# The opening of a decoder trunk: one accumulator per group of modulation columns, and scaling and rounding on ScalarE

## The chip, the cores and the metric

The kernel runs on one core of one Trainium2 chip. TensorE (PE) multiplies matrices, its loads of the stationary operand stand as PEld; Vector (DVE), ScalarE (ACT) and GpSimd (POOL) work on elements; SyncE (SP) issues every transfer here. Each engine runs its own queue in order and waits on semaphores for the others. The metric is device time in microseconds (us) of one execution. Before the change three runs took 1229.35 to 1232.19, median 1229.94.

## The reference

A trunk of two layers on 256 tokens of width 1024, all in float32. Every sublayer normalizes x, changes it by a shift and a scale that come from a vector c, computes (SwiGLU with 2816 hidden columns, attention, SwiGLU again), and adds a gated result to x. The part that this case is about is the start of the first SwiGLU:

```python
c_act = silu(c)
mod = (c_act @ mod_w[0] + mod_b[0])          # 9 vectors of 1024; shift and scale are the first two
h = rms_norm(x, norm_g) * (1 + scale) + shift
gate, up = h @ w_gate, h @ w_up              # then silu(gate) * up, and the product with w_down
```

## The kernel before, in words

Each float32 operand of a large product is kept as two parts: a rounded one (hTh for h, wh for weights) and the residue (hTl, wl). ScalarE rounds a weight tile of 128 x 1024 numbers, Vector subtracts to get the residue, and TensorE makes three products: wh with hTh, wh with hTl, wl with hTh.

The opening (open_trunk, line 672) must have h before it can multiply. It takes the 1024 input features in four groups of two columns of 128 (groups, k0 and n). For a group q, load_mod loads the rows of mod_w for shift and scale of these 256 features, eight tiles of 128 x 512 numbers (256 KB each, tag oraw), and load_weights loads three tiles of 512 KB: for each feature column k one with 512 columns of gate and 512 of up (key (0, k)), and one for both columns with the next 512 of gate (key (1, k), k even). The tag raw has four such tiles (RAWS).

reduce (line 751) multiplies the eight mod_w tiles by the eight columns of c and adds them up on Vector, in two accumulators (k even, k odd). modulate (line 763) sums each accumulator over its 128 partitions with TensorE, by matmuls with a column of ones; a float32 matmul of this kind shows as two instructions, so a group has sixteen. Then Vector makes shift and scale (tile sb) and h itself (hk), ScalarE rounds it to hTh, Vector makes hTl. split (line 739) rounds a weight tile and makes its residue. normalize (line 700) squares x on ScalarE, takes the root on GpSimd, scales x on Vector (tile u), transposes it on TensorE and copies it to xT on ScalarE. columns (line 685) turns rows into columns by one transpose and a Vector copy: for c, and for gain, shift bias and scale bias (gb8).

products (line 793) makes the twelve matmuls of a piece: one feature column k against 512 weight columns, in four blocks of 128, three kinds of product for each (mm_blocks, line 383). pieces lists a group's six: the gate and up halves of (0, k), those of (0, k+1), then the two columns of (1, k). The outputs stand in six PSUM banks until the end of the opening; two banks are left for transposes and column sums.

The order on every engine is the order in which the program writes the instructions: in the opening it is kept on PE, SP, DVE, ACT and POOL. For group q it is: the remaining reduces of q, the column sums, the first weight splits (OPEN_SPLIT of them, between), shift, scale and h, first reduces of q+1 (OPEN_MEAN, meanwhile), residues of h, the other splits, reduces of q+1 up to OPEN_HEAD; on TensorE the sums, the pieces held back of group q-1 (backlog, OPEN_HOLD: 3, 2, 2), then the pieces of q but for those held back. Behind the opening a planner orders DVE, ACT and POOL, and an instruction written later can come to run inside the opening. weights.start (line 191) begins the loads of the next phase when group 3 is reached.

Of the kernel before, what the change touches and what calls it, by code (L numbers as in the profile page):

```python
# [17 lines left out]
P = 128  # L18
# [6 lines left out]
H = 16  # L25
# [5 lines left out]
OPEN_HEAD = 4  # L31
OPEN_SPLIT = (2, 2, 2, 1)
OPEN_MEAN = (1, 2, 2)
OPEN_HOLD = (3, 2, 2)
# [57 lines left out]
def trunk_kernel(ctx, tc, x_in, c_in, positions, mod_w, mod_b, norm_g, w_gate, w_up, w_down,  # L92
# [62 lines left out]
    nc.gpsimd.memset(ones.bitcast(F32), 1.0)  # L155

# [228 lines left out]
    def mm_blocks(o, k, wh, wl, first, last):  # L385

        for i in range(4):
# [3 lines left out]
            pe.matmul(out_i, wl[:, blk], hTh[:, :, k, :], start=False, stop=last and i % 2 == 1)  # L391

# [278 lines left out]
    def open_trunk(wg, wu, pool):  # L671
# [28 lines left out]
        def normalize(t):  # L700
            ss = main.tile([P, 2], F32, tag="ss", bufs=4, name="ss")
            for h in range(2):
                square(t, h, slice(h * 512, (h + 1) * 512), ss)
            rs = rms_scale(ss)

            def half(h):
                xn = main.tile([P, 512], F32, tag="u", bufs=3, name="u")
                dve.tensor_scalar(xn, x[t][:, h * 512:(h + 1) * 512], rs, None, op0=OP.mult)
                tp = bank4()
                for k in range(4):  # L710
                    pe.transpose(tp[:, k, :], xn[:, k * P:(k + 1) * P], ident)
                act.copy(xT[:, t, h * 4:(h + 1) * 4, :], tp)

            return [lambda: half(0), lambda: half(1)]
# [10 lines left out]

        def load_weights(q):
            k0, n = groups[q]
            for k in range(k0, k0 + n):
                rows = slice(k * P, (k + 1) * P)
                raw = rawp.tile([P, 2, 512], F32, tag="raw", bufs=RAWS, name="raw")  # L730
# [3 lines left out]
                if k % 2 == 0:  # L734
                    raw = rawp.tile([P, 2, 512], F32, tag="raw", bufs=RAWS, name="raw")
                    nc.sync.dma_start(raw, wg[k * P:(k + 2) * P, 512:1024].rearrange("(k p) n -> p k n", p=P))
                    ws[1, k] = raw

        def split(key):
# [4 lines left out]
            dve.tensor_sub(wl, raw, wh.bitcast(F32))  # L744
            ws[key] = wh, wl
            uses[key] = 2
            weights.live += 1

        accs = {}

        def reduce(q, rows, extra=()):
            n = groups[q][1]
            for k in rows:
                if k < 2:
                    accs[q, k] = pool.tile([P, 2, 2 * P], F32, tag=f"cacc{k}", bufs=2, name=f"cacc{k}")[:, :, 0:n * P]
                    dve.tensor_scalar(accs[q, k], raws[q, k], ccol[:, k:k + 1], None, op0=OP.mult)
                else:
                    dve.scalar_tensor_tensor(accs[q, k % 2], raws[q, k], ccol[:, k:k + 1], accs[q, k % 2],
                                                   op0=OP.mult, op1=OP.add)
                if extra:  # L760
                    extra.pop(0)()

        def modulate(q, between, meanwhile):
            k0, n = groups[q]
            cp = bank()
            terms = [(accs[q, i], ones.bitcast(F32)[:, 0:1]) for i in range(2)]
            for j in range(2):
                for i in range(n):
                    for m, (a, c) in enumerate(terms):
                        pe.matmul(cp[:, n * j + i:n * j + i + 1], a[:, j, i * P:(i + 1) * P], c,  # L770
                                         start=m == 0, stop=m == len(terms) - 1)
            between()
# [5 lines left out]
            hk = pool.tile([P, NT, 2, P], F32, tag="hk", bufs=2, name="hk")  # L778
            for i in range(n):
                dve.tensor_scalar(hk[:, :, i, :], xT[:, :, k0 + i], sb[:, 1, i:i + 1], sb[:, 0, i:i + 1],  # L780
                                        op0=OP.mult, op1=OP.add)
            for t in range(NT):
                act.copy(hTh[:, t, ks, :], hk[:, t, 0:n])  # L783
            meanwhile()
# [633 lines left out]
```

## Time and profile before

| | |
|---|---|
| median of three runs | 1229.94 us |
| the profiled execution | 1230.24 us, its span 1228.5 us |
| TensorE busy | 1202.4 us, 98% |
| Vector busy | 936.6 us, 76% |
| ScalarE busy | 657.4 us, 54% |
| transfers | 281 MB, 229 GB/s over the span |

Times are counted from the start of the span. A busy TensorE is not TensorE at its peak: its matmuls overlap, so the pace, from one start to the next, says more than the duration of one. In a row of the timeline, the bracket is the idle time of that engine before the instruction and what released it.

### The profile page before, as it was taken

The numbers are of one execution on the slowest core, as the hardware profiler recorded it, in microseconds if no ns is written. First come the engines' busy times: TensorE is split into PE (matmuls) and PEld (weight loads), VectorE is DVE, ScalarE is ACT, GpSimd is POOL, SyncE is SP. The second block draws the span as 40 slices with busy tenths as digits, with TensorE's granted clock in tenths as the row PEclk, the third lists the DMA queues.
The fourth block names the chain that finished last, engine by engine and source line by source line (L and its number), as shares of the span: only waits on it lengthen the run. The fifth ranks groups of instructions, "written<-read, shape, count | busy, mean of one in ns | idle before, by whom it ended". The sixth has DMA issues, their size and how long they took to land.

```text
span 1228.5 us, 21017 instructions
## 1 busy us (share of the span) xinstructions
PE 1202.4 (98%) x8130; PEld 1085.5 (88%) x8130; DVE 936.6 (76%) x1318; ACT 657.4 (54%) x1002; POOL 101.9 (8%) x130
## 2 busy tenths in 40 slices
PE   6999999999999999999999999999999999999998
PEld 5999988878779999889999887888888787999987
DVE  7878777998788887579978659978686877765653
ACT  4446444676654554444554435677575665544540
POOL 1000000222100000000000003131131200000000
PEclk9999999999999999999999999999999999999999
DMA  9879885695739988638888647656545552866461
GB/s 334 277 269 327 304 317 182 199 306 201 272 99 341 330 275 310 206 111 292 305 277 325 206 154 235 210 181 211 175 154 182 197 173 86 289 203 217 168 213 42
DMA packets 152069, 281.21 MB, mean 229 GB/s; under 512 B 13424, under 2 KB 79504, under 8 KB 151968
## 3 DMA queue, kind: packets, MB, share of 16 engines
q1 hardware_dynamic: 151968, 279.85, 68.4%
q8 instruction: 64, 1.05, 0.3%
q14 instruction: 37, 0.30, 0.1%
HBM read 277.71 MB, written 2.10 MB: 228 GB/s over the span
## 4 chain that ended last, share of the span: by engine, by line
PE 76%; DVE 9%; DMA 5%; issue 4%; POOL 2%; ACT 2%; SPq 0%; POOLq 0%; DVEq 0%; ACTq 0%
PE block_bank L389 13%; PE block_bank L391 13%; PE block_bank L390 13%; PE bank L394 11%; PE bank L395 11%; PE bank L396 11%; DMA mraw<-in_mod_w_dram 3%; DVE wl L215 2%; POOL hrs L860 2%; DVE acc L296 1%; DVE lo L924 1%; PE obank L949 1%; DMA raw<-in_dil_w_in_dram 1%; DMA raw<-in_fox_w_in_dram 1%; ACT wh L206 1%
## 5 line engine op out<-in xcount | busy, mean ns | idle before, releaser
L215 DVE TENSOR_TENSOR wl<-raw,wh 128x1024 fp32r<-128x1024 f32 (+1 forms) x360 | 434.9, 1216 | 160.1 <-ACT wh L206 156.8
L206 ACT CAST wh<-raw 128x1024 fp32r<-128x1024 f32 (+1 forms) x360 | 374.5, 1046 | 299.2 <-PE bank L396 107.2
L389 PE MATMUL block_bank<-hTh,wh 128*128 128x256 f32 x1312 | 371.6, 283 | 2.0 <-ACT hTh L783 2.0
L391 PE MATMUL block_bank<-hTh,wl 128*128 128x256 f32 x1312 | 371.4, 283 | 0.0
L390 PE MATMUL block_bank<-hTl,wh 128*128 128x256 f32 x1312 | 370.7, 283 | 0.0
L389 PEld LDWEIGHTS block_bank<-hTh,wh 128*128 128x128 f32 x1312 | 248.5, 189 | 2.5 <-ACT hTh L783 2.1
L390 PEld LDWEIGHTS block_bank<-hTl,wh 128*128 128x128 f32 x1312 | 248.2, 189 | 0.5 <-DVE hTl L786 0.2
L391 PEld LDWEIGHTS block_bank<-hTh,wl 128*128 128x128 f32 x1312 | 248.0, 189 | 0.0
L394 PE MATMUL bank<-wh,hTh 128*128 128x512 f32 (+2 forms) x496 | 192.0, 387 | 0.8 <-DVE nm L924 0.8
L396 PE MATMUL bank<-wh,hTl 128*128 128x512 f32 (+2 forms) x496 | 181.6, 366 | 0.0
L395 PE MATMUL bank<-wl,hTh 128*128 128x512 f32 (+2 forms) x496 | 181.0, 365 | 0.0
L296 DVE SCALAR_TENSOR_TENSOR acc<-mraw,ccols,acc 128x1024 f32<-128x1024 f32 x112 | 143.4, 1281 | 29.8 <-DMA mraw<-in_mod_w_dram 29.3
L395 PE MATMUL bank<-wl,aTh 128*128 128x512 f32 (+1 forms) x420 | 146.4, 349 | 0.0
L394 PE MATMUL bank<-wh,aTh 128*128 128x512 f32 (+1 forms) x420 | 146.1, 348 | 0.0
L396 PE MATMUL bank<-wh,aTl 128*128 128x512 f32 (+1 forms) x420 | 145.7, 347 | 0.0
L396 PEld LDWEIGHTS bank<-wh,hTl 128*128 128x128 f32 x496 | 93.2, 188 | 16.5 <-DVE hTl L471 0.5
L394 PEld LDWEIGHTS bank<-wh,hTh 128*128 128x128 f32 x496 | 93.6, 189 | 14.0 <-DVE nm L924 1.2
L395 PEld LDWEIGHTS bank<-wl,hTh 128*128 128x128 f32 x496 | 93.7, 189 | 12.3
L394 PEld LDWEIGHTS bank<-wh,aTh 128*128 128x128 f32 x420 | 79.5, 189 | 10.8
L396 PEld LDWEIGHTS bank<-wh,aTl 128*128 128x128 f32 x420 | 79.3, 189 | 10.5
L395 PEld LDWEIGHTS bank<-wl,aTh 128*128 128x128 f32 x420 | 79.5, 189 | 10.1
L926 ACT ACTIVATE lo<-lo,nm 128x128 f32<-128x128 f32 (+1 forms) x64 | 37.8, 591 | 64.8 <-DVE nm L924 64.7
(225 smaller groups left out, 1280.9 us busy)
## 6 DMA issues: line engine op xcount, KB each, us to landing
mraw<-in_mod_w_dram SPq DMA_DIRECT2D x128, 512.0 KB, 5.2
raw<-in_ffn_w_down_dram SPq DMA_DIRECT2D x88, 512.0 KB, 4.1
raw<-in_ffn_w_gate_dram SPq DMA_DIRECT2D x76, 512.0 KB, 4.4
raw<-in_ffn_w_up_dram SPq DMA_DIRECT2D x76, 512.0 KB, 4.6
raw<-in_dil_w_in_dram SPq DMA_DIRECT2D x128, 256.0 KB, 4.2
raw<-in_fox_w_in_dram SPq DMA_DIRECT2D x36, 256.0 KB, 4.8
oraw<-in_mod_w_dram SPq DMA_DIRECT2D x32, 256.0 KB, 6.3
raw<-in_ffn_w_gate_dram SPq DMA_DIRECT2D x24, 256.0 KB, 6.0
```

Source lines behind the costliest of these rows:

```text
L206: act.copy(wh, self.raws[self.hi])
L215: dve.tensor_sub(wl, self.raws[self.lo], wh.bitcast(F32))
L296: dve.scalar_tensor_tensor(acc, raw, ccol[:, k:k + 1], self.bias_tile if k == 0 else acc, op0=OP.mult, op1=OP.add)
L389: pe.matmul(out_i, wh[:, blk], hTh[:, :, k, :], start=first and i % 2 == 0, stop=False)
L390: pe.matmul(out_i, wh[:, blk], hTl[:, :, k, :], start=False, stop=False)
L391: pe.matmul(out_i, wl[:, blk], hTh[:, :, k, :], start=False, stop=last and i % 2 == 1)
L394: pe.matmul(o, ah, wh, start=first, stop=False)
L395: pe.matmul(o, ah, wl, start=False, stop=False)
L396: pe.matmul(o, al, wh, start=False, stop=last)
L860: nc.gpsimd.tensor_tensor(rs, ms, mhalf, op=OP.pow)
L924: dve.tensor_tensor_reduce(out=lo[:, 0:n], in0=lg[:, 0:n], in1=m, scale=-1.0, scalar=BIG, op0=OP.add, op1=OP.min, accum_out=nm)
L926: act.activation(lo[:, 0:n], lo[:, 0:n], AF.Exp, bias=nm, scale=-1.0, accum_out=sums[:, t, i:i + 1])
```

## The change

What it does, part by part. reduce adds all eight tiles of a group into one accumulator; for groups 1 to 3 the first multiplication runs on ScalarE. The column sums have half as many passes. normalize scales x on ScalarE and copies up to three transposed halves later. The copy of the gain and bias columns is written behind the reduce of k = 4 of group 0. modulate, now a generator, rounds h on ScalarE straight from xT; the plain h is made by Vector in group 0 and by ScalarE in the others; residues of h are made by column. Splits are cut in two (split_hi on ScalarE, split_lo on Vector), and the adds of the next group are written between the residues of the weights: two ahead of each in groups 1 and 2, all behind them in group 0. Every third raw tile of the opening comes from a new tag with two tiles. Within a piece the matmuls are ordered by kind (mm_parts). One piece of each group is held back. A small constant (idr) is built at the front of the kernel.

```diff
@@ -28,10 +28,7 @@
...
 OPEN_GROUPS = (2, 2, 2, 2)
-OPEN_HEAD = 4
-OPEN_SPLIT = (2, 2, 2, 1)
-OPEN_MEAN = (1, 2, 2)
-OPEN_HOLD = (3, 2, 2)
+OPEN_HOLD = 1
 T_FOX = 2
@@ -154,6 +151,11 @@
...
+    idr = const.tile([CUM, H], F32R, name="idr")
+    nc.gpsimd.memset(idr.bitcast(F32), 0.0)
+    for r in (0, 2 * H):
+        dve.tensor_copy(idr[r:r + H, :], ident[r:r + H, r:r + H])
     mhalf = const.tile([P, 8], F32, name="mhalf")
@@ -389,6 +391,14 @@
...
             pe.matmul(out_i, wl[:, blk], hTh[:, :, k, :], start=False, stop=last and i % 2 == 1)
+    def mm_parts(o, k, wh, wl, first, last):
+        for w, h in ((wh, hTh), (wh, hTl), (wl, hTh)):
+            for i in range(4):
+                blk = slice(i * P, (i + 1) * P)
+                pe.matmul(o[i // 2][:, i % 2], w[:, blk], h[:, :, k, :], start=first and w is wh and h is hTh and
+                          i % 2 == 0, stop=last and w is wl and i % 2 == 1)
@@ -697,21 +707,27 @@
...
-        def normalize(t):
-            ss = main.tile([P, 2], F32, tag="ss", bufs=4, name="ss")
-            for h in range(2):
-                square(t, h, slice(h * 512, (h + 1) * 512), ss)
-            rs = rms_scale(ss)
-            def half(h):
-                xn = main.tile([P, 512], F32, tag="u", bufs=3, name="u")
-                dve.tensor_scalar(xn, x[t][:, h * 512:(h + 1) * 512], rs, None, op0=OP.mult)
-                tp = bank4()
-                for k in range(4):
-                    pe.transpose(tp[:, k, :], xn[:, k * P:(k + 1) * P], ident)
-                act.copy(xT[:, t, h * 4:(h + 1) * 4, :], tp)
-            return [lambda: half(0), lambda: half(1)]
+        def normalize():
+            rs = []
+            for t in range(NT):
+                ss = main.tile([P, 2], F32, tag="ss", bufs=4, name="ss")
+                for h in range(2):
+                    square(t, h, slice(h * 512, (h + 1) * 512), ss)
+                rs.append(rms_scale(ss))
+            held = []
+            for t in range(NT):
+                for h in range(2):
+                    xn = main.tile([P, 512], F32, tag="u", bufs=3, name="u")
+                    act.activation(xn, x[t][:, h * 512:(h + 1) * 512], AF.Copy, scale=rs[t])
+                    tp = bank4()
+                    for k in range(4):
+                        pe.transpose(tp[:, k, :], xn[:, k * P:(k + 1) * P], ident)
+                    held.append((xT[:, t, h * 4:(h + 1) * 4, :], tp))
+                    if len(held) == 3:
+                        act.copy(*held.pop(0))
+            for dst, tp in held:
+                act.copy(dst, tp)
@@ -723,67 +739,78 @@
...
                     raws[q, k + i] = one
+        raw_n = [0]
+        def opening_raw():
+            raw_n[0] += 1
+            if raw_n[0] % 3 == 0:
+                return pool.tile([P, 2, 512], F32, tag="raw2", bufs=2, name="raw2")
+            return rawp.tile([P, 2, 512], F32, tag="raw", bufs=RAWS, name="raw")
         def load_weights(q):
             k0, n = groups[q]
             for k in range(k0, k0 + n):
                 rows = slice(k * P, (k + 1) * P)
-                raw = rawp.tile([P, 2, 512], F32, tag="raw", bufs=RAWS, name="raw")
+                raw = opening_raw()
                 nc.sync.dma_start(raw[:, 0], wg[rows, 0:512])
                 nc.sync.dma_start(raw[:, 1], wu[rows, 0:512])
                 ws[0, k] = raw
                 if k % 2 == 0:
-                    raw = rawp.tile([P, 2, 512], F32, tag="raw", bufs=RAWS, name="raw")
+                    raw = opening_raw()
                     nc.sync.dma_start(raw, wg[k * P:(k + 2) * P, 512:1024].rearrange("(k p) n -> p k n", p=P))
                     ws[1, k] = raw
-        def split(key):
+        def split_hi(key):
             raw = ws[key]
             wh = wp.tile([P, 2, 512], F32R, tag="wh", name="wh")
             wl = wp.tile([P, 2, 512], F32R, tag="wl", name="wl")
             act.copy(wh, raw)
-            dve.tensor_sub(wl, raw, wh.bitcast(F32))
-            ws[key] = wh, wl
+            ws[key] = wh, wl, raw
             uses[key] = 2
             weights.live += 1
+        def split_lo(key):
+            wh, wl, raw = ws[key]
+            dve.tensor_sub(wl, raw, wh.bitcast(F32))
         accs = {}
-        def reduce(q, rows, extra=()):
+        def reduce(q, k):
             n = groups[q][1]
-            for k in rows:
-                if k < 2:
-                    accs[q, k] = pool.tile([P, 2, 2 * P], F32, tag=f"cacc{k}", bufs=2, name=f"cacc{k}")[:, :, 0:n * P]
-                    dve.tensor_scalar(accs[q, k], raws[q, k], ccol[:, k:k + 1], None, op0=OP.mult)
+            if k == 0:
+                accs[q] = pool.tile([P, 2, 2 * P], F32, tag="cacc", bufs=2, name="cacc")[:, :, 0:n * P]
+                if q:
+                    act.activation(accs[q], raws[q, k], AF.Copy, scale=ccol[:, k:k + 1])
                 else:
-                    dve.scalar_tensor_tensor(accs[q, k % 2], raws[q, k], ccol[:, k:k + 1], accs[q, k % 2],
-                                                   op0=OP.mult, op1=OP.add)
-                if extra:
-                    extra.pop(0)()
-        def modulate(q, between, meanwhile):
+                    dve.tensor_scalar(accs[q], raws[q, k], ccol[:, k:k + 1], None, op0=OP.mult)
+            else:
+                dve.scalar_tensor_tensor(accs[q], raws[q, k], ccol[:, k:k + 1], accs[q], op0=OP.mult, op1=OP.add)
+        def modulate(q):
             k0, n = groups[q]
             cp = bank()
-            terms = [(accs[q, i], ones.bitcast(F32)[:, 0:1]) for i in range(2)]
             for j in range(2):
                 for i in range(n):
-                    for m, (a, c) in enumerate(terms):
-                        pe.matmul(cp[:, n * j + i:n * j + i + 1], a[:, j, i * P:(i + 1) * P], c,
-                                         start=m == 0, stop=m == len(terms) - 1)
-            between()
+                    pe.matmul(cp[:, n * j + i:n * j + i + 1], accs[q][:, j, i * P:(i + 1) * P],
+                              ones.bitcast(F32)[:, 0:1], start=True, stop=True)
             ks = slice(k0, k0 + n)
             sb = pool.tile([P, 2, 2], F32, tag="sb", bufs=4, name="sb")
...
             dve.tensor_mul(sb[:, 1, 0:n], sb[:, 1, 0:n], g00[:, ks])
             dve.tensor_add(sb[:, 0, 0:n], cp[:, 0:n], shift_b[:, ks])
-            hk = pool.tile([P, NT, 2, P], F32, tag="hk", bufs=2, name="hk")
+            hk = pool.tile([P, 2, NT, P], F32, tag="hk", bufs=2, name="hk")
             for i in range(n):
-                dve.tensor_scalar(hk[:, :, i, :], xT[:, :, k0 + i], sb[:, 1, i:i + 1], sb[:, 0, i:i + 1],
-                                        op0=OP.mult, op1=OP.add)
-            for t in range(NT):
-                act.copy(hTh[:, t, ks, :], hk[:, t, 0:n])
-            meanwhile()
-            for t in range(NT):
-                dve.tensor_sub(hTl[:, t, ks, :], hk[:, t, 0:n], hTh[:, t, ks, :].bitcast(F32))
+                act.activation(hTh[:, :, k0 + i, :], xT[:, :, k0 + i], AF.Identity, scale=sb[:, 1, i:i + 1],
+                               bias=sb[:, 0, i:i + 1])
+                if q:
+                    act.activation(hk[:, i], xT[:, :, k0 + i], AF.Identity, scale=sb[:, 1, i:i + 1],
+                                   bias=sb[:, 0, i:i + 1])
+                else:
+                    dve.tensor_scalar(hk[:, i], xT[:, :, k0 + i], sb[:, 1, i:i + 1], sb[:, 0, i:i + 1],
+                                      op0=OP.mult, op1=OP.add)
+                yield lambda i=i: dve.tensor_sub(hTl[:, :, k0 + i, :], hk[:, i], hTh[:, :, k0 + i, :].bitcast(F32))
         def pieces(q):
@@ -792,9 +819,9 @@
...
             w, wk, i, o = piece
-            wh, wl = ws[w, wk]
+            wh, wl, _ = ws[w, wk]
             k = wk + (i if w else 0)
-            mm_blocks(outs[o], k, wh[:, i], wl[:, i], k == 0, k == KT - 1)
+            mm_parts(outs[o], k, wh[:, i], wl[:, i], k == 0, k == KT - 1)
             uses[w, wk] -= 1
@@ -805,40 +832,43 @@
...
         nq = len(groups)
-        head, rest = range(0, OPEN_HEAD), range(OPEN_HEAD, KT)
         load_mod(0, range(KT))
         load_weights(0)
-        halves = normalize(0) + normalize(1)
-        reduce(0, range(KT), halves)
-        columns(gb8, 3, gbcol)
+        normalize()
+        for k in range(KT):
+            reduce(0, k)
+            if k == 4:
+                columns(gb8, 3, gbcol)
         backlog = []
         for q in range(nq):
-            todo = keys(q)
+            units, more = keys(q), range(0)
             if q:
                 load_weights(q)
-                reduce(q, rest)
-            def between():
-                for _ in range(OPEN_SPLIT[q]):
-                    if todo:
-                        split(todo.pop(0))
-            def meanwhile():
-                if q + 1 < nq:
-                    load_mod(q + 1, range(KT))
-                    reduce(q + 1, range(OPEN_MEAN[q]))
-            modulate(q, between, meanwhile)
-            while todo:
-                split(todo.pop(0))
+            split_hi(units[0])
+            lows = modulate(q)
+            next(lows)()
+            split_lo(units[0])
+            for low in lows:
+                low()
+            for u in units[1:]:
+                split_hi(u)
             if q + 1 < nq:
-                reduce(q + 1, range(OPEN_MEAN[q], OPEN_HEAD))
-            else:
+                load_mod(q + 1, range(KT))
+                reduce(q + 1, 0)
+                more = range(1, KT)
+            early = 2 if q else 0
+            for i, u in enumerate(units[1:]):
+                for k in more[early * i:early * (i + 1)]:
+                    reduce(q + 1, k)
+                split_lo(u)
+            for k in more[early * (len(units) - 1):]:
+                reduce(q + 1, k)
+            if q + 1 == nq:
                 weights.start()
...
             todo = pieces(q)
-            cut = len(todo) if q == nq - 1 else max(0, len(todo) - OPEN_HOLD[q])
+            cut = len(todo) if q == nq - 1 else len(todo) - OPEN_HOLD
             for piece in todo[:cut]:
...
```

The part left out takes the three lines that build idr from fox_tables, and its name from the tuple that hands it on.

## Rows read from the trace of the kernel before

**Rows 1.** Stretches: us; busy (count) PE, PEld, DVE, ACT, POOL; PE clock, DMA share, GB/s.

```profile
0.00:19.85 19.85, 8.61 (x34) 6.78 (x34) 12.05 (x28) 9.67 (x20) 5.61 (x27) 1.00 0.93 318
19.85:61.55 41.70, 41.70 (x336) 41.50 (x337) 36.87 (x63) 18.53 (x25) 0.00 (x0) 1.00 0.89 299
61.55:1228.50 1166.95, 1152.11 (x7763) 1037.24 (x7761) 887.70 (x1229) 629.17 (x959) 96.29 (x103) 1.00 0.68 225
```

**Rows 2.** TensorE's waits: us in total, times, longest us.

```profile
PE obank L949 <- DVE on L966: 1.7, 1, 1.7
```

**Rows 3.** The chain of waits from 0 to 28: start us, us, what.

```profile
6.23 1.34 ACT junk L401 x4
...
14.67 3.16 PE bank L770 x14
...
19.85 0.58 PE block_bank L389
...
24.34 0.21 PE block_bank L389
...
24.67 0.12 PE block_bank L391
```

**Rows 4.** Timeline of TensorE and its weight loads: start us, us, engine, line, instruction.

```profile
12.03 0.71 PEld L711 LDWEIGHTS bank<-ident,u 128*128 128x128 f32 x4 [0.34 <-DVE u L708]
...
13.07 0.30 PE L687 MATMUL bank<-ident,gb 24*128 24x24 f32 x1
...
26.41 1.84 PE L770 MATMUL bank<-ones,cacc 128*128 128x1 f32 x16
...
50.18 0.37 PE L389 MATMUL block_bank<-hTh,wh 128*128 128x256 f32 x1
```

**Rows 5.** L389, a third of the products, in group 3: us; busy PE, PEld; clock.

```profile
50.15:61.55 11.40, 9.06 (x32) 6.04 (x33) 1.00 0.67 217
```

**Rows 6.** Timeline of Vector in the opening.

```profile
7.68 0.49 DVE L756 TENSOR_SCALAR cacc<-oraw,ccols 128x512 f32<-128x512 f32 x1
...
14.63 0.33 DVE L1026 CAST idr<-ident 16x16 fp32r<-16x16 f32 x2
...
22.32 4.06 DVE L758 SCALAR_TENSOR_TENSOR cacc<-oraw,ccols,cacc 128x512 f32<-128x512 f32 x6
26.29 2.35 DVE L744 TENSOR_TENSOR wl<-raw,wh 128x1024 fp32r<-128x1024 f32 x2
...
40.03 0.16 DVE L775 SCALAR_TENSOR_TENSOR sb<-bank,gbcol 128x2 f32<-128x2 f32 x1 [1.07 <-PE bank L770]
...
40.31 0.15 DVE L777 TENSOR_TENSOR sb<-bank,gbcol 128x2 f32<-128x2 f32 x1
```

**Rows 7.** ScalarE by line and form: count, busy us, mean ns, idle us before.

```profile
L926 ACT ACTIVATE lo<-lo,nm 128x512 f32<-128x512 f32 x32 | 23.2, 724 | 42.9 <-DVE nm L924 42.9
...
L955 ACT COPY wide<-ri 128x512 f32<-128x512 f32 x7 | 4.3, 613 | 2.0 <-DVE ri L953 2.0
...
L783 ACT CAST hTh<-hk 128x256 fp32r<-128x256 f32 x8 | 2.9, 405 | 15.6 <-DVE hk L780 15.6
...
L677 ACT ACT_TABLE_LOAD x1 | 1.3, 1283 | 0.8 <-PEq L1398 0.8
```

**Rows 8.** Timeline of ScalarE in the opening.

```profile
45.04 1.05 ACT L743 CAST wh<-raw 128x1024 fp32r<-128x1024 f32 x1 [2.11 <-DMA raw<-in_ffn_w_up_dram]
...
52.20 2.00 ACT L743 CAST wh<-raw 128x1024 fp32r<-128x1024 f32 x2
```

**Rows 9.** Timeline of Vector behind the opening.

```profile
71.37 1.28 DVE L296 SCALAR_TENSOR_TENSOR acc<-mraw,ccols,bias 128x1024 f32<-128x1024 f32 x1
72.68 1.28 DVE L296 SCALAR_TENSOR_TENSOR acc<-mraw,ccols,acc 128x1024 f32<-128x1024 f32 x1
```

**Rows 10.** Instructions of two tiles: duration ns min/median/max, first and last start.

```profile
L758 DVE SCALAR_TENSOR_TENSOR cacc<-oraw,ccols,cacc x24: 737/744/878, 9.6 to 47.4; 128x512 f32<-128x512 f32 x24
...
L786 DVE TENSOR_TENSOR hTl<-hk,hTh x8: 417/418/426, 19.5 to 52.4; 128x256 fp32r<-128x256 f32 x8
```

More of the change, by code (lines that the diff above doesn't have):

```diff
@@ L1022, in fox_tables @@
         nc.gpsimd.memset(neg1, -1.0)
-        idr = const.tile([CUM, H], F32R, name="idr")
-        nc.gpsimd.memset(idr.bitcast(F32), 0.0)
-        for r in (0, 2 * H):
-            dve.tensor_copy(idr[r:r + H, :], ident[r:r + H, r:r + H])
         gcol = const.tile([P, 2], F32, name="fgcol")
@@ L1036, in fox_tables @@
         dve.scalar_tensor_tensor(gain, gcol[:, 0:1], HD ** -0.5, gcol[:, 1:2], op0=OP.mult, op1=OP.mult)
-        tabs["fox"] = masks, tri, neg1, idr, gain, bf
+        tabs["fox"] = masks, tri, neg1, gain, bf
     def plan_fox():
@@ L1050, in fox @@
         weights.spare = pool, "xwh", "xwl"
-        masks, tri, neg1, idr, gain, bf = tabs["fox"]
+        masks, tri, neg1, gain, bf = tabs["fox"]
         done = set()
```

## The prediction

> **What bounds the kernel now.** I read the span by stretches first, then TensorE's waits, the chain of the opening, and the opening engine by engine. TensorE has work in 1202 of 1228.5 us: only what starts its stream earlier, shortens it or opens a hole in it moves the time. Of the 26 us without work, 11.2 lie ahead of 19.85, none between 19.85 and 61.55, and 14.8 are spread over the other 1167 us [rows 1], in waits of at most 1.7 us [rows 2]. So the opening is 19.85 us of getting started and then a full stream to 61.55.
>
> The chain shows how the start comes about: behind the Vector adds of group 0's columns, column-sum passes take from 14.67 to 17.83, then come shift and scale, h and its rounding, and the first product stands at 19.85 [rows 3]. The granted clock is 1.00 in every stretch [rows 1], but the pace shows two levels: a product matmul every 0.21 us up to 24.34 (1.2 GHz), every 0.12 from 24.67 (2.4 GHz) [rows 3]; 96 of the latter in 11.4 us give 0.119 [rows 5]. It changes after 4.5 us of products without a break, in which some 21 were done. I take the same behind the new start.
>
> Vector is the second engine to watch: group 1's adds end at 26.38 [rows 6], and TensorE turns to their sums at 26.41 [rows 4]. The opening has almost no spare Vector time.
>
> **The start.** Each sum is made in the profiled execution, 1230.24 us around a span of 1228.5; the median shown is 0.3 lower. Scaling x leaves Vector for ScalarE. There an instruction that reads a per-partition operand does not cost what a copy costs: 512 columns take 0.724 us with one against 0.613 without [rows 7], so 0.72 each. The first follows the squares, done at 7.57 [rows 3], and ends at 8.25. Sixteen transposes on TensorE, 0.26 each (four from 12.03 to 13.07 [rows 4]), end at 12.5; the transpose of the gain and bias columns stands behind them, 0.30, to 12.8. Vector meanwhile runs one chain of dependent adds. Independent adds follow each other every 0.664 us (six in 4.06 [rows 6]); one that reads the result of the one before starts 0.03 after that one's end: 71.37 to 72.68 is 1.31 for an instruction of 1.28 [rows 9]. At 0.744 [rows 10] a chained add costs 0.775. From 7.68 the first multiply (0.49) and four adds end at 11.3. There the copy of the columns is now written into the chain, and it must wait for TensorE's 12.8: 1.6 us are lost. Three more adds end at 15.25; now they end ahead of 14.67. Eight sum passes at 0.226 (fourteen in 3.16 [rows 3]) end at 17.05, shift and scale take 0.43 (40.03 to 40.46 [rows 6]). h is now rounded straight from x: 256 columns cost 0.405 without a per-partition operand [rows 7], and for a scale and a bias I add 0.11 each, 0.61 (ends: 0.40 as if they were free, 0.72 as for 512 columns). First product at 18.2, 1.65 us earlier.
>
> **Up to the sums of group 1.** Vector's order behind shift and scale (17.5) is: h and its residue for one column (0.42 each [rows 10]), a weight residue, the second column, two weight residues, then seven chained adds. A weight residue is 1.13 (two in 2.35 [rows 6]). That is 22.8 for the residues and 28.1 for the last add. TensorE has 60 products before these sums (one piece of twelve is held back, it was three): 21 at the slow pace and 39 at 0.119 end at 27.3. It waits 0.8 and ends the sums at 29.0 (eight passes, 0.92, half of sixteen's 1.84 [rows 4]). Now they end at 28.25, but with 24 products fewer done, 2.85 us. The lead is 2.85 - 0.75 = 2.1 us.
>
> **Groups 1 and 2, the step that decides.** Count from the end G of a group's sums. TensorE: the held piece, 1.42, then four matmuls of column k with the rounded h and weights, to G+1.9. Shift and scale are done at G+0.5. On ScalarE now come two instructions per column (h rounded, h plain), 0.61 long and 0.52 apart, then two weight roundings, 0.96 apart (two in 2.00 [rows 8]), and only then the first multiply of the next group: it ends at G+5.3. On Vector: residue of h, G+2.1; weight residue of column k, G+3.3; then the order written in the new loop: two chained adds (they wait for the G+5.3), a weight residue, two adds, and only then the weight residue of column k+1: 6.85, 7.95, 9.4, 10.5. But TensorE needs that one third: its two pieces of column k end at G+5.2, eight matmuls of column k+1 at G+6.1, and the next four read it. The hole is 4.4 us. Smaller ones stand ahead: the residues of h and of column k come at G+2.1 and G+3.3 where TensorE could use them at G+1.9 and G+2.4, 0.9 in all. So a group lasts 0.92 + 72 x 0.119 + 0.9 + 4.4 = 14.8 us; now the two take 21.9 together, from 28.25 to 50.18 [rows 4].
>
> Weights are not late in this: a rounding that waits for its transfer stands at 45.04 now, the last such wait of the opening [rows 8], and the products that want it come at 58.6. Group 3 has no adds behind it, so only the 0.9.
>
> **The sum.** Lead at group 1: -2.1. Two more groups of sums, eight passes less in each: -1.85. Holes: 0.9 x 3 + 4.4 x 2 = +11.5. Together +7.6; by the clock, the opening ends at 29.0 + 2 x 14.8 + 84 x 0.119 + 0.9 = 69.5 where 61.55 stands now, +7.9. I take +7.8: 1238.0 beside the profiled 1230.24, or 1237.7 beside the median.
>
> Costed at nothing: the two more raw tiles. They let two loads of the next phase leave before the last residues of the opening are done, but TensorE waits for no weight there (none idle up to 61.55 [rows 1]) and gains nothing; SyncE issues the same transfers in the same order. The constant tile moved to the front is two Vector copies, 0.33 [rows 6], ahead of any data. The new order of a piece (four matmuls of a kind at a time) has the same twelve. Behind the opening, Vector has its last residue done 4.8 us before the last product, so I forecast no second loss; without that cover it would be the price of one residue, 1.2.
>
> Identity is a function that this trace does not run. Silu, Square and Copy share one table load in the opening, 1.283 us [rows 7]; two more would add up to 2.6; I take none, as for Square and Copy. The Trainium skill ("ScalarE: Activation LUTs", Table sets: the hidden batching unit) says that cheap functions, identity among them, stand in every set, which would be the none; no row here shows it.
>
> Both ends of the rest: if chained adds overlapped like independent ones, the opening would end at 64.6 (+3.1); with per-partition operands free too, at 63.0 (+1.5), and with the columns' copy not waiting as well, at 61.0 (-0.5). If each add took its longest, 0.878 [rows 10], it would end at 72 (+10.5).
>
> **Rivals.** (1) Faster: Vector does not follow the written order, and the residue of column k+1 comes before the adds. For: the constant tile's two copies, written far behind the opening, ran inside it at 14.63 [rows 6]. Against: every other Vector instruction of the opening stands as written. It decides if that residue ends by G+6.1; then Vector's own work sets the pace, 10.1 us a group (7 x 0.775, 3 x 1.13, 1.3 for the rest), or TensorE's: the opening ends between 60 and 57.5, -1.5 to -4, so 1227. (2) No change: the chain costs less than its rows, the lower ends above, 1231. (3) Slower still: the clock falls in the holes. TensorE's longest wait at the fast level is 1.7 us [rows 2]; a hole of 4.4 is not shown. If both cost a new 4.5 us at the slow pace, 21 matmuls losing 0.094 each, that is +2.0 for each: 1242. The Trainium skill ("TensorE: Matmul & The Clock Gate", HAM oscillation — how this bites in real kernels) describes just that, a stream of matmuls put back to the low clock by each wait for its next data; no wait of this trace is long enough to try it.
>
> **How the numbers follow.** Forecast 0.69 (1233 to 1241 by itself), clock 0.10, no change 0.10, faster 0.11. About 0.2%, 2.5 us, is what a measurement of this kernel can tell from no change. Slower 0.80: the forecast, the clock and 0.01 of the second rival; same 0.09; faster 0.11. The range 1229.5 to 1241.5 leaves out the first rival and most of the third.
>
> **What would show it.** Right: the first product near 18.2; the copy of the gain columns near 12.9 inside the chain of adds; TensorE idle for 4 to 5 us, twice, ahead of the third kind of matmul of columns 3 and 5, with the Vector residue as releaser; column sums of groups 2 and 3 near 43 and 58, eight passes each. Wrong: no TensorE idle beyond 1 us between 20 and 60, sums about 10 us apart, or adds 0.66 apart.

## The result: 0.9% slower, all of it in the opening

The changed kernel takes 1240.5 us (median of 4 runs, 1239.99 to 1243.62) where the kernel before takes 1230.68 (median of 4 runs on the same chip): a ratio of 1.0088, 95% interval 1.0076 to 1.0100, slower. The profiled execution took 1240.39 us with a span of 1238.7, 10.15 us more than that of before. The forecast was +7.8. The two holes that it named are in the trace; so is a fall of TensorE's clock behind each of them, which its sum left out.

The stretches of the changed kernel (busy us and count of PE, PEld, DVE, ACT, POOL; granted clock; DMA share; GB/s), cut at the first product, at the first product of the next phase, and at the two places where the clock is low:

```profile
0.00:16.91 16.91, 5.44 (x27) 5.00 (x27) 8.34 (x20) 10.84 (x22) 5.09 (x27) 0.93 0.88 309
16.91:71.78 54.87, 44.37 (x313) 42.55 (x314) 38.04 (x56) 24.53 (x34) 0.00 (x0) 0.90 0.75 245
71.78:1238.70 1166.92, 1151.94 (x7762) 1038.04 (x7760) 888.67 (x1231) 629.86 (x961) 94.98 (x103) 1.00 0.68 225
...
38.57:42.09 3.52, 3.52 (x17) 3.52 (x18) 2.11 (x3) 0.00 (x0) 0.00 (x0) 0.52 1.10 352
...
54.95:58.85 3.90, 3.90 (x20) 3.90 (x21) 2.12 (x3) 0.00 (x0) 0.00 (x0) 0.59 0.12 47
```

Against [rows 1]: what follows the opening takes 1166.92 us where it took 1166.95, so all of the loss lies ahead of 71.78, which was 61.55: +10.23. The start is 2.94 shorter (16.91 against 19.85); the stream of products is 13.17 longer (54.87 against 41.70), and TensorE, which had work in all of it, now has none in 10.5 us of it.

TensorE in the opening (start us, us, engine, line, instruction, and in brackets the idle time before it with its releaser):

```profile
14.22 1.48 PE L796 MATMUL bank<-ones,cacc 128*128 128x1 f32 x8 [2.51 <-DVE cacc L788]
16.91 1.22 PE L400 MATMUL block_bank<-hTh,wh 128*128 128x256 f32 x4 [1.21 <-ACT hTh L805]
...
27.99 0.73 PE L400 MATMUL block_bank<-hTh,wh 128*128 128x256 f32 x4
...
33.84 0.64 PE L400 MATMUL block_bank<-hTl,wh 128*128 128x256 f32 x4
38.57 1.23 PE L400 MATMUL block_bank<-hTh,wl 128*128 128x256 f32 x4 [4.09 <-DVE wl L775]
...
42.09 0.64 PE L400 MATMUL block_bank<-hTh,wh 128*128 128x256 f32 x4
...
44.32 0.73 PE L400 MATMUL block_bank<-hTh,wh 128*128 128x256 f32 x4
...
54.95 0.75 PE L400 MATMUL block_bank<-hTh,wl 128*128 128x256 f32 x4 [4.09 <-DVE wl L775]
...
56.29 1.06 PE L400 MATMUL block_bank<-hTl,wh 128*128 128x256 f32 x4
...
60.70 0.72 PE L400 MATMUL block_bank<-hTh,wh 128*128 128x256 f32 x4
...
71.78 0.28 PE L391 MATMUL block_bank<-hTh,wh 128*128 128x256 f32 x1
```

There are two holes of 4.09 us, one ahead of the third kind of product of column 3, the other ahead of that of column 5, both released by Vector's weight residue. Behind the first the pace is half at once: sixteen matmuls from 38.57 to 42.09 are 0.22 us each, where the next ones are 0.119. Behind the second it falls some six matmuls later, and the row at 56.29 is at half pace. The granted clock of these two stretches is 0.52 and 0.59 of 2.4 GHz. Why the residue is late stands in Vector's row order:

```profile
33.25 1.54 DVE L788 SCALAR_TENSOR_TENSOR cacc<-oraw,ccols,cacc 128x512 f32<-128x512 f32 x2 [1.60 <-ACT cacc L784]
34.71 1.22 DVE L775 TENSOR_TENSOR wl<-raw,wh 128x1024 fp32r<-128x1024 f32 x1
35.85 1.53 DVE L788 SCALAR_TENSOR_TENSOR cacc<-oraw,ccols,cacc 128x512 f32<-128x512 f32 x2
37.30 1.22 DVE L775 TENSOR_TENSOR wl<-raw,wh 128x1024 fp32r<-128x1024 f32 x1
```

Vector first waits 1.60 us for the first multiply on ScalarE, then does two adds, a residue that nobody needs yet, two more adds, and only then the residue (37.30) for which TensorE has stood since 34.5 (33.84 and 0.64).

### The profile page after: what moved, and what is told of

It reads as the page before. It is cut to its first block, busy times and chain, and to the rows that moved or that the text cites. A ratio compares the mean times of both kernels' runs of the same rounds, so it can differ in the third digit from the quotient of the medians.

```text
span 1238.7 us, 20963 instructions
## 1 busy us (share of the span) xinstructions
PE 1201.7 (97%) x8098; PEld 1085.6 (88%) x8098; DVE 935.1 (75%) x1305; ACT 665.2 (54%) x1015; POOL 100.1 (8%) x130
## 4 chain that ended last, share of the span: by engine, by line
PE 80%; DVE 7%; DMA 5%; ACT 3%; issue 3%; POOL 2%; SPq 0%; POOLq 0%; DVEq 0%; ACTq 0%
PE bank L404 12%; PE bank L405 12%; PE bank L406 12%; PE block_bank L393 12%; PE block_bank L391 12%; PE block_bank L392 12%; DVE wl L217 2%; PE block_bank L400 2%; PE obank L979 1%; DMA mraw<-in_mod_w_dram 1%; DMA raw<-in_dil_w_in_dram 1%; PE bank L966 1%; POOL hrs L890 1%; ACT wh L208 1%; PE bank L1325 1%
## 5 line engine op out<-in xcount | busy, mean ns | idle before, releaser
L393 PE MATMUL block_bank<-hTh,wl 128*128 128x256 f32 x1216 | 344.3, 283 | 0.0
L391 PE MATMUL block_bank<-hTh,wh 128*128 128x256 f32 x1216 | 344.1, 283 | 0.0
L392 PE MATMUL block_bank<-hTl,wh 128*128 128x256 f32 x1216 | 343.2, 282 | 0.0
L391 PEld LDWEIGHTS block_bank<-hTh,wh 128*128 128x128 f32 x1216 | 229.8, 189 | 0.3
L392 PEld LDWEIGHTS block_bank<-hTl,wh 128*128 128x128 f32 x1216 | 229.6, 189 | 0.4
L393 PEld LDWEIGHTS block_bank<-hTh,wl 128*128 128x128 f32 x1216 | 229.3, 189 | 0.0
L406 PEld LDWEIGHTS bank<-wh,aTl 128*128 128x128 f32 x420 | 79.3, 189 | 10.5
```

The costliest lines, as they stand in the source:

```text
L391: pe.matmul(out_i, wh[:, blk], hTh[:, :, k, :], start=first and i % 2 == 0, stop=False)
L392: pe.matmul(out_i, wh[:, blk], hTl[:, :, k, :], start=False, stop=False)
L406: pe.matmul(o, al, wh, start=False, stop=last)
```

## The experiments

Each was timed beside the kernel before on the same chip. "Opening's end" is the first product of the next phase: 61.55 in the kernel before, 71.78 in the changed one.

### All adds behind the residues

```
-            early = 2 if q else 0
+            early = 0
```

> The changed kernel with one word of its order on VectorE undone: none of the next group's chained adds stands ahead of the weight residues of this group; all seven stand behind them. Theory A (VectorE's written order makes the holes: four adds of 1.31 us stand between the residue of the second key and that of the third, and TensorE waits 4.09 us for it): both holes of 4.1 us go, TensorE's clock does not fall in groups 1 and 2, and the column sums of groups 1 and 2 come late instead, by about 1.8 us each. The next phase's first product then starts at about 63.5 us instead of 71.78, and the run takes about 1232 us. Theory B (the chain through a single accumulator is what costs: each add waits for the one before): the chain now starts later, so the sums come later by as much as the holes give back, and the run takes 1240 us or more.

Measured: 1233.6 us, ratio 1.0028 (1.0018 to 1.0038). TensorE in it:

```profile
39.37 1.02 PE L796 MATMUL bank<-ones,cacc 128*128 128x1 f32 x8 [1.76 <-DVE cacc L788]
40.25 0.72 PE L400 MATMUL block_bank<-hTh,wh 128*128 128x256 f32 x4
...
51.89 1.09 PE L796 MATMUL bank<-ones,cacc 128*128 128x1 f32 x8 [1.77 <-DVE cacc L788]
52.85 1.20 PE L400 MATMUL block_bank<-hTh,wh 128*128 128x256 f32 x4
...
64.45 0.28 PE L391 MATMUL block_bank<-hTh,wh 128*128 128x256 f32 x1
```

Both long holes are gone, the sums wait 1.8 us instead, and the opening ends 7.3 us earlier with the same chain of adds. One number in Vector's order makes 0.0060 of the 0.0088. The clock held in groups 1 and 2, as expected; it fell once, behind the wait for the sums of group 3 (1.20 us for four products from 52.85, 0.72 from 40.25).

### The holes filled with work for TensorE

```
+            if w is wl and fill:
+                idle = block_bank()
+                for n in range(fill):
+                    pe.matmul(idle[:, 0], wh[:, 0:P], hTh[:, :, k, :], start=True, stop=True)
...
```

> The changed kernel with 32 products whose result nobody reads, put into TensorE's stream ahead of the third kind of product of the pieces at which the two long holes stand (32 x 0.11 us = 3.5 us of the 4.09 us). They wait for nothing that is late, so the holes stay as long as VectorE makes them. Theory C (the granted clock falls to half in each hole, and the 15 to 17 products behind it at 0.22 us instead of 0.11 us are a cost of their own beside the hole): the clock stays at 1.00 in groups 1 and 2, the opening ends 3.0 us earlier (1.6 us for each hole, less what small gaps cost), and the run takes about 1237.4 us. Theory A alone (only the length of the wait counts, and the next group's sums are bound by VectorE's adds): no change, 1240.4 us, since the slow products would end before the next wait of TensorE anyway. If the added products are themselves at half speed, they end behind the hole and the run is above 1241 us.

Measured: 1238.73 us, ratio 1.0063 (1.0049 to 1.0076).

```profile
28.51 0.72 PE L404 MATMUL block_bank<-hTh,wh 128*128 128x256 f32 x4
...
34.84 3.96 PE L401 MATMUL block_bank<-hTh,wh 128*128 128x256 f32 x32
39.08 0.73 PE L404 MATMUL block_bank<-hTh,wl 128*128 128x256 f32 x4 [0.28 <-DVE wl L779]
...
43.31 0.73 PE L404 MATMUL block_bank<-hTh,wh 128*128 128x256 f32 x4
...
58.18 0.73 PE L404 MATMUL block_bank<-hTh,wh 128*128 128x256 f32 x4
...
69.25 0.28 PE L391 MATMUL block_bank<-hTh,wh 128*128 128x256 f32 x1
```

Vector's residue comes as late as ever, but the products behind it run at full pace. A group, from the first product behind its sums (28.51) to that of the next, takes 14.80 and 14.87 us where it took 16.33 and 16.38: the clock is a term of its own, 1.5 us for each hole, 3.0 together. Theory C holds.

### The second column's first half ahead of the wide second half

```
+            units = [units[0], units[2], units[1]]
```

> The changed kernel with the order of the second and third key of each group exchanged: the weights of the second column's first half come ahead of those of the wide second half, and so do their rounding and residue. Nothing else moves: two adds still stand ahead of each of the last two residues. Theory A: the residue that TensorE needs first now has two adds ahead of it and not four, the hole falls from 4.1 us to about 1.7 us, the sums of groups 1 and 2 come about 1.4 us late, the opening ends near 66.2 us, and the run takes about 1235 us. Theory B (the single accumulator's chain): the chain ends at the same time as before, so the sums and the run stay, 1240 us.

Measured: 1237.19 us, ratio 1.0060 (1.0047 to 1.0074).

```profile
35.88 0.75 PE L400 MATMUL block_bank<-hTh,wl 128*128 128x256 f32 x4 [1.50 <-DVE wl L775]
...
40.79 1.02 PE L796 MATMUL bank<-ones,cacc 128*128 128x1 f32 x8 [1.29 <-DVE cacc L788]
41.67 1.11 PE L400 MATMUL block_bank<-hTh,wh 128*128 128x256 f32 x4
...
67.10 0.28 PE L391 MATMUL block_bank<-hTh,wh 128*128 128x256 f32 x1
```

The holes are 1.50 and 1.08 us and the sums' waits 1.29 and 1.32, as theory A has it; theory B falls. The opening ends 4.7 us earlier than in the changed kernel, where 5.6 were expected: the clock falls anyway, behind both waits of the sums (1.11 us for four products from 41.67). By the ratios the gain is only 3.4 us. The six executions run from 1233.77 to 1240.04; the trace is of the one at 1233.77, and what the others lost, no trace shows.

### Two accumulators again

```
...
-                dve.scalar_tensor_tensor(accs[q], raws[q, k], ccol[:, k:k + 1], accs[q], op0=OP.mult, op1=OP.add)
+                dve.scalar_tensor_tensor(accs[q, k % 2], raws[q, k], ccol[:, k:k + 1], accs[q, k % 2],
+                                         op0=OP.mult, op1=OP.add)
...
```

> The changed kernel with two accumulators for each group again, as in the kernel before: adds alternate between them, so that no add waits for the one just ahead of it, and the column sums take 16 products instead of 8. The order on VectorE stays as changed, but for the second row, which is now a product without an add. Theory A: four adds still stand ahead of the third residue, and they are shorter by about 0.1 us each, so the hole shrinks from 4.1 us to about 3.4 us; the sums take about 1 us longer for each of the four groups; together +1.4 us, about 1242 us. Theory B (the single accumulator costs the time): the opening falls back to about that of the kernel before, and the run takes about 1231 us.

Measured: 1241.19 us, ratio 1.0083 (1.0070 to 1.0095), the changed kernel's time within the intervals. Theory B falls: without the chain the holes stay, 3.17 and 3.18 us where theory A had 3.4.

```profile
38.27 0.74 PE L400 MATMUL block_bank<-hTh,wl 128*128 128x256 f32 x4 [3.17 <-DVE wl L775]
...
54.63 0.74 PE L400 MATMUL block_bank<-hTh,wl 128*128 128x256 f32 x4 [3.18 <-DVE wl L775]
55.22 0.64 PE L400 MATMUL block_bank<-hTh,wh 128*128 128x256 f32 x4
```

### The opening's order written anew

```
-                reduce(q + 1, 0)
-                more = range(1, KT)
+                more = range(KT)
...
+            if q + 1 < nq:
+                load_weights(q + 1)
+                split_hi(keys(q + 1)[0])
+                split_lo(keys(q + 1)[0])
```

> The changed kernel with its opening's order written anew, all else kept: the first key's rounding and residue of the next group stand behind this group's adds, so that they are done before its column sums are; the second column's first half comes ahead of the wide second half; the unrounded h and the first multiply of the chain go back to VectorE (0.41 us and 0.49 us there, against 0.59 us and 0.72 us on ScalarE), so that no chain waits for ScalarE to come round. Theory A (all of the loss is VectorE's written order): the three short waits for the first residue (0.40 us) and both long holes go, sums start near 27.4, 38.3 and 49.3 us, the next phase's first product at about 59.3 us against 61.55 us in the kernel before, and the run takes about 1228 us. Theory D (VectorE has too much work in this form whatever its order: eight rows, three residues, four passes over h are 11.8 us a group, more than the 9.5 us of products and sums): the sums come late in each group by more than the model says, and the opening ends at 61.5 us or later, the run at 1230 us or above.

Measured: 1230.42 us, ratio 0.9994 (0.9984 to 1.0005): the whole loss is undone with the single accumulator and the new start kept. But it does not pass the kernel before: the 0.9 us by which its opening ends earlier (60.67) lies within the interval.

```profile
27.29 0.99 PE L793 MATMUL bank<-ones,cacc 128*128 128x1 f32 x8
...
38.53 1.02 PE L793 MATMUL bank<-ones,cacc 128*128 128x1 f32 x8 [1.36 <-DVE cacc L785]
...
40.44 1.05 PE L400 MATMUL block_bank<-hTh,wl 128*128 128x256 f32 x4
...
49.73 1.02 PE L793 MATMUL bank<-ones,cacc 128*128 128x1 f32 x8
...
60.67 0.28 PE L391 MATMUL block_bank<-hTh,wh 128*128 128x256 f32 x1
```

Theory A is right on the order: both long holes are gone, and the sums start within 0.5 us of its places. But they stand 11.2 us apart, and Vector works from 26 to 52 us with one pause of 0.19, which is theory D's point; and the clock fell once more (four products in 1.05 us at 40.44). The opening ends between A's 59.3 and D's 61.5, and A's 1228 us is missed.

### The start alone, on the kernel before

```
-                dve.tensor_scalar(xn, x[t][:, h * 512:(h + 1) * 512], rs, None, op0=OP.mult)
...
+                    act.activation(xn, x[t][:, h * 512:(h + 1) * 512], AF.Copy, scale=rs[t])
...
```

> The kernel before with the changed start alone: x scaled on ScalarE for both tiles behind the squares, transposes behind it, and the small columns copied inside the chain of adds. Two accumulators, VectorE's and TensorE's order of the groups as before. Theory A (the start is a gain that the groups behind it lose again by their new order): the first product starts at about 18.2 us instead of 19.85 us, and since TensorE waits for nothing in groups 1 to 3 of the kernel before and VectorE starts earlier by the same, the lead is kept: about 1228.4 us, 1.6 us under the kernel before. Theory E (the lead is worth nothing since the sums of group 1 are bound by something that doesn't move, the arrival of the columns or VectorE's chain): sums of group 1 stay at 26.4 us and the run at 1230 us.

Measured: 1229.86 us, ratio 0.9994 (0.9985 to 1.0004).

```profile
13.85 3.81 PE L776 MATMUL bank<-ones,cacc 128*128 128x1 f32 x16 [1.96 <-DVE cacc L764]
...
19.69 0.58 PE L389 MATMUL block_bank<-hTh,wh 128*128 128x256 f32 x1 [2.03 <-ACT hTh L789]
```

The sums of group 0 begin 0.16 us earlier, and so does the first product: theory A's 1.6 us is refuted. Theory E is not tested, as there was no lead to lose. Scaling x on ScalarE brings next to nothing with the rest as it was. Part of that is the constant tile idr, whose copies fell into the chain of adds here and waited 0.88 us for GpSimd; but two weight residues stand on Vector ahead of the scale and end at 17.52, and the scale starts at 17.70, so that without those copies it could have come no more than 0.2 us earlier.

### The start with one accumulator

```
-                if k < 2:
+                if k == 0:
...
```

> The same start, and one accumulator for each group in place of two: 8 sums instead of 16, each add waiting for the one ahead of it. The order of VectorE and TensorE in the groups stays as in the kernel before. Theory A: the chained adds cost VectorE about 0.8 us more for a group (seven of 0.75 us and one of 0.48 us against six of 0.67 us and two of 0.48 us), the sums cost TensorE 0.9 us less for each of groups 1 to 3 and about 1.1 us less at the start; VectorE comes just in time for group 1 in the kernel before, so most of that group's gain is lost there: the first product near 17.1 us, the opening's end near 57 us instead of 61.55 us, and the run near 1225.5 us. Theory B (the single accumulator is what costs): no better than the kernel before, 1230 us or more.

Measured: 1230.78 us, ratio 0.9996 (0.9987 to 1.0005). Theory A's 1225.5 us is out. Theory B's forecast, no better than the kernel before, is met, and the trace shows why. TensorE, then Vector:

```profile
14.39 1.86 PE L773 MATMUL bank<-ones,cacc 128*128 128x1 f32 x8 [2.66 <-DVE cacc L764]
...
26.96 1.05 PE L773 MATMUL bank<-ones,cacc 128*128 128x1 f32 x8 [1.48 <-DVE cacc L764]
```

```profile
14.96 2.51 DVE L750 TENSOR_TENSOR wl<-raw,wh 128x1024 fp32r<-128x1024 f32 x2 [0.63 <-ACT wh L749]
17.39 0.15 DVE L778 SCALAR_TENSOR_TENSOR sb<-bank,gbcol 128x2 f32<-128x2 f32 x1
```

The eight sums end at 16.25, 1.4 us ahead of the sixteen; but two residues stand on Vector ahead of the scale, which starts at 17.39 all the same. The sums of group 1 then wait 1.48 us for the longer chain, where they waited for nothing [rows 4], and the granted clock is 0.53 from 29.40 to 33.00: what eight sums fewer save, this takes back. So in the old order the longer chain does cost something; the holes of the changed kernel it does not make.

### One residue ahead of the scale

```
-OPEN_SPLIT = (2, 2, 2, 1)
+OPEN_SPLIT = (1, 2, 2, 1)
```

> The run of the start with one accumulator, with one number changed: one residue of weights stands on VectorE ahead of the scale and shift of group 0, not two. Theory A (whatever stands on VectorE ahead of the small operations that TensorE waits for sets the time): in that run the sums of group 0 end at 16.25 us, but the scale starts at 17.39 us, behind the second residue; with one residue ahead it starts at about 16.25 us and the first product at about 18.2 us instead of 19.37 us. VectorE's work up to the sums of group 1 stays the same, so these move by less, from 26.96 us to about 26.5 us, and the run by no more than 0.5 us. Rival: the first product does not move, since it waits for the rounding of h on ScalarE, which then makes way for another rounding of weights.

Measured: 1230.82 us, ratio 1.0002 (0.9993 to 1.0011). The scale now starts as soon as the sums are done (17.23), but these come 0.9 us later than in the run above. 0.6 of it is the constant tile: its copies, which the kernel before ran behind its chain [rows 6], fell into the chain of adds and waited there for GpSimd, 0.88 us instead of 0.24. Vector, then TensorE:

```profile
10.91 0.43 DVE L1030 CAST idr<-ident 16x16 fp32r<-16x16 f32 x2 [0.88 <-POOL idr L1028]
...
17.23 0.16 DVE L778 SCALAR_TENSOR_TENSOR sb<-bank,gbcol 128x2 f32<-128x2 f32 x1 [0.65 <-PE bank L773]
```

```profile
19.23 0.58 PE L389 MATMUL block_bank<-hTh,wh 128*128 128x256 f32 x1 [2.04 <-ACT hTh L786]
```

The first product came at 19.23, not 18.2; whether it would have without that wait stays open. So of the 2.94 us by which the changed kernel starts earlier, three runs with some of its parts got 0.16, 0.48 and 0.62. What none of them has is h rounded straight from x: TensorE waits 2.04 us for it here and 1.21 in the changed kernel. The rest of the 2.94, 2.1 us, lies in the sums of group 0, which end at 15.70 in the changed kernel and at 17.82 in the one before.

### Adds in the gap of h, on the new order

```
-            for low in list(modulate(q)):
-                low()
+            lows = list(modulate(q))
...
+            adds(3 if q else 0)
+            for low in lows:
+                low()
...
```

> The order of the run with the first key ahead, with two more edits. The unrounded h of groups 1 to 3 goes to ScalarE again (0.73 us less on VectorE for a group), and while ScalarE makes h, VectorE does the first multiply and two adds of the next group, which stand ahead of the residues of h; one more add stands ahead of the second residue of weights and four ahead of the third. Two of the six pieces of products are held back over the next sums instead of one. Theory D (in that run VectorE, with no idle time from 26 to 52 us, set the period of 11.2 us between the sums): the period falls to about 10 us, the sums of groups 2 and 3 start near 36.6 and 46.8 us instead of 38.53 and 49.73 us, the opening ends at about 59.1 us instead of 60.67 us, and the run takes 1.6 us less than that one, about 1.8 us less than the kernel before (1228.9 us). If something else set the period (TensorE's own products, the loads), it stays at 11.2 us and the run at that of the kernel before.

Measured: 1229.16 us, ratio 0.9988 (0.9978 to 0.9997): under the kernel before and, by the two ratios, 1.0% under the changed one.

```profile
26.94 1.05 PE L793 MATMUL bank<-ones,cacc 128*128 128x1 f32 x8 [1.81 <-DVE cacc L785]
...
28.42 1.05 PE L400 MATMUL block_bank<-hTl,wh 128*128 128x256 f32 x4
...
38.06 0.95 PE L793 MATMUL bank<-ones,cacc 128*128 128x1 f32 x8
...
47.50 0.95 PE L793 MATMUL bank<-ones,cacc 128*128 128x1 f32 x8
...
59.79 0.28 PE L391 MATMUL block_bank<-hTh,wh 128*128 128x256 f32 x1
```

From group 2 to 3 the period is 9.44 us where it was 11.2, so Vector's work and its order had set it, as theory D has it; which of the edits made in this run brought it is not shown. From group 1 to 2 it is 11.12: the wait of 1.81 us ahead of the sums at 26.94 put the clock down for the next 20 or so products. The opening ends at 59.79, 0.7 later than expected for that.

## Why the prediction came out 2.4 us short

**The direction and the place were right.** The profiled executions differ by 10.15 us where the forecast had 7.8. The two holes stand at the two places named, with Vector's weight residue as releaser: 4.09 us by the bracket and 4.25 by the starts (33.84 to 38.57 less four products) where 4.4 stood. The sums of groups 2 and 3 start at 43.51 and 59.89 where 43 and 58 stood. Moving the adds (first run) shows that this order is the cause, and not the chain of adds (fourth run). One thing was not tried by itself: the changed kernel holds back one piece of a group, where the kernel before holds back three and two. Each further piece would put 1.42 us of products (12 x 0.119) ahead of the hole.

**The step that was mis-sized is "Groups 1 and 2".** It gave a group 14.8 us with TensorE's products at 0.119 throughout. They take 16.33 and 16.38; with the holes filled and the clock held they take 14.80 and 14.87. So the step's own terms fit within 0.1, and the missing term, put at nothing, is the clock behind each hole: 32.7 us for the two, less 29.7, is 3.0 us. The text had it as its third rival, 1242 us, +2.0 for each hole at a chance of 0.10, and that is what happened. The price was somewhat high (measured 1.5 for each); the chance was too small. Once the clock was up, no wait in the trace of before was longer than 1.7 us [rows 2], and the products behind that one, at 1021.67, are at full pace; so its rows could not show what 4 us do, and the sum took silence for "no". The Trainium skill ("TensorE: Matmul & The Clock Gate", HAM oscillation — how this bites in real kernels) describes a kernel whose every wait for its next data puts TensorE back to the low clock. The trace after agrees at both holes; the run with two accumulators does not at its second hole of 3.18 us.

**"The start" and "Up to the sums of group 1" were 1.0 us too slow.** The sums of group 1 ended at 27.99, not 29.0. The copy of the gain columns stands in the chain of adds as said, but it ran at 11.75, not 12.9, and the last add of group 0 ended at 14.17, not 15.25: the sixteen transposes took 0.22 us each and began 0.25 us earlier (8.00, not 8.25). The 0.26 that was used was a misreading: four weight loads took 0.71 us, to 12.74, and the text counted up to the next instruction at 13.07 [rows 4]. The first product came at 16.91, forecast 18.2.

**The unit prices held.** ScalarE and Vector, by line (busy us, mean ns of one, idle before):

```profile
L788 DVE SCALAR_TENSOR_TENSOR cacc<-oraw,ccols,cacc 128x512 f32<-128x512 f32 x22 | 16.5, 751 | 3.7 <-ACT cacc L784 3.2
...
L805 ACT ACTIVATE hTh<-xT,sb 128x256 fp32r<-128x256 f32 x8 | 4.7, 594 | 24.6 <-DVE sb L802 24.6
...
L784 ACT ACTIVATE cacc<-oraw,ccols 128x512 f32<-128x512 f32 x3 | 2.2, 719 | 0.0
```

An instruction that makes h with scale and bias took 0.594 us, where 0.61 was taken between 0.40 and 0.72; the multiply took 0.719, where 0.72 was taken. Seven chained adds take 5.47 us, 0.787 apart, where 0.775 was taken: the second rival (a cheaper chain) is out. No new table load stands in the opening. The Trainium skill ("ScalarE: Activation LUTs", Table sets: the hidden batching unit) has cheap functions, identity among them, in every set, and the trace agrees: one load, at 0.78 us, as before. The first rival (Vector out of its written order) is out too: the adds and residues above stand as written.

**The sum, closed.** In opening's ends, 69.5 forecast: -1.0 (start) +3.0 (clock) +0.2 (group 3 took 11.08 us for 10.9) = 71.7; measured 71.78. These are two errors of opposite sign: the better start, which was not foreseen, hid a third of the clock's cost.

## What to carry to other kernels

Write the order of a shared engine by when its consumer needs each result: here four adds, for sums that began at 43.51, stood ahead of one residue that TensorE had wanted since 34.5. A shorter instruction stream or an earlier start was worth nothing here where the same queue held the next small operation behind something long (the runs of the start). When a forecast opens holes in a TensorE stream that had none, add a clock term for each of them in the sum itself.

## What the runs showed of the hardware

The clock did not follow the length of the wait. It fell behind both holes of 4.09 us; of the two holes of 3.17 and 3.18 us (two accumulators) it fell behind the first alone (the products from 55.22 are at full pace); and it fell behind much shorter waits when the column sums stood next: 1.29, 1.32, 1.36, 1.48, 1.77 and 1.81 us, though not behind those of 1.76 and 2.10. It did not fall behind the holes of 1.50 and 1.08 us that stood ahead of products (second column first). Behind which waits it falls is not settled by these runs. A fall cost 1.5 us behind each of the two long holes, by the run that filled them.
